# Attention scores as two products over 128 partitions, with the high and low parts stacked inside SBUF

## The chip, the cores and the metric

The kernel runs on one core of one Trainium2 chip. The metric is the device time of one execution in microseconds (us). Before the change the median of three runs is 1916.58 us, the lowest 1916.14 and the highest 1916.92. One execution was also taken by the hardware profiler; its own time is 1916.25 us, and the profile's span, from its first to its last instruction, is 1914.5 us.

## The reference

The program is a small decoder trunk on 512 tokens of width 1024, all in 32-bit floats. Its first layer is a SwiGLU half step, a short gated convolution and a second SwiGLU half step. Keys and values are then projected once from the residual stream. Its second layer is a SwiGLU half step, a causal differential attention over those keys and values, and a last SwiGLU half step. Each sub-layer stands between two RMS norms. The change lies wholly in the attention:

```
k, v = split(rms_norm(x, g_kv) @ w_kv, 2)       # k: 8 heads x 2 x 64,  v: 8 heads x 128
q = (h @ w_q).reshape(b, s, 8, 2, 64) * 64**-0.5
scores = einsum("bqhcd,bkhcd->bhcqk", q, k)     # c = 0, 1: two score matrices in each head
p = softmax(where(causal, scores, -inf))
a = p[:, :, 0] - lam * p[:, :, 1]
o = rms_norm(einsum("bhqk,bkhe->bqhe", a, v), g_subln) * (1 - lambda_init)
m = o.reshape(b, s, 1024) @ w_o
```

So each of the 8 heads has two score matrices of 512 x 512, each a contraction over 64 features; they are masked, normalised row by row, mixed into one matrix, and applied to the head's values.

## The kernel before, in words

**Products in parts.** TensorE multiplies operands of the type fp32r. To keep 32-bit accuracy every operand is held as two tiles: `hi`, the value cast to fp32r by ScalarE (ACT), and `lo`, the remainder, subtracted by VectorE (DVE). The helper `split` (L136) makes both. A product is three matmuls into one PSUM bank: hi by hi, hi by lo, lo by hi (`products`, L143). Weights come in units of 128 x 1024 (512 KB): `unit` (L119) loads a raw tile from the queue of SyncE (SP), ACT casts it to `whi` (L128), DVE subtracts `wlo` (L129). There are two raw tiles, so the load after next waits until DVE has read the raw tile. The pairs `whi`/`wlo` lie in a pool of seven pairs (`wsp`, WUNITS = 7); `pair_of_units` (L112) takes one pair.

**The attention stage.** The queries of all heads are projected first, into the tiles `q`. Then, in `body` (L711 to L750):

- `values(0)` and `values(1)` project the values, four weight units each, 96 matmuls of 512 columns each (L618 to L620).
- `queries(n)` splits one head's queries. It takes a pair from the weight pool: the left halves of the two tiles hold query hi and lo, the right halves will hold key hi and lo.
- `keys(n, k0, k1)` multiplies one weight unit, 24 matmuls of 512 columns for a whole head, and at the end splits the result into the right halves of that pair. In those tiles partitions 0 to 63 belong to the score matrix c = 0 and partitions 64 to 127 to c = 1.
- `scores(n, qt)` makes both score matrices of a block of 128 queries against the keys up to the diagonal, w = (qt + 1) x 128 columns. For each of the three pairs of parts there are two matmuls, one over partitions 0 to 63 and one over 64 to 127 (L653); then one bf16 matmul per matrix adds the causal mask (L655). DVE takes the row maximum (L656), ACT the exponential with the row sum (L661), DVE the reciprocal (L662), ACT scales the second matrix (L665), and DVE mixes the two (L666).
- `turn(n, qt)` transposes the mixed block on TensorE (L678) and splits it; `attend(n)` multiplies it with the values; `sub_norm(n)` normalises the result; `normed` splits it for the output projection.
- `wo.begin(m, ks)` starts column block m of the output projection with the input blocks ks: three matmuls of 512 columns for each.

Before the loop stand values(0), queries(0), keys(0), values(1) and scores(0, 3). Iteration n of the loop makes the keys of head n + 1 in two halves, between them and after them the scores of head n, the transposes, and the attention of head n - 1. The matmuls of the keys, and in the last iteration those of `wo.begin`, are what TensorE has to do while the softmax of a block runs on DVE and ACT. After the loop come the last head, the rest of the output projection and its norm (`closing`, L256).

**What sets the order.** The code names the order in which work is recorded; a scheduler in the tile framework then interleaves the instructions of each engine. What runs on an engine is a fixed list, and each engine works through its list strictly in turn. A tile that is asked for from a pool takes a slot in the order of the code.

## Time and profile before

| what | value |
|---|---|
| median of three runs | 1916.58 us (1916.14 to 1916.92) |
| the profiled execution, its own time | 1916.25 us |
| the profile's span | 1914.5 us |
| TensorE busy over the span | 1895.8 us (99%) |
| DVE, ACT busy over the span | 993.3 us (52%), 739.5 us (39%) |
| granted TensorE clock | 0.999 |

In the views below PE is TensorE's matmuls, PEld its weight loads, SP the queue of SyncE. A row of the timeline gives the start in us, the duration in us, the engine, the line, the operation, output and inputs, the shape and the number of merged instructions, and in brackets how long the engine had been idle and what ended that. A matmul's duration holds the time until its result has left the array; matmuls that follow one another overlap, so the rate is read from the distance between two starts. A row of the table by stretches has the stretch, its length, and for PE, PEld, DVE, ACT and POOL the busy time with the number of instructions, then the granted clock, the DMA share and GB/s.

The stages that the text speaks of, by the trace's own clock: values(0) from 1333.66, keys(0) from 1355.42, values(1) from 1360.86, the first scores at 1382.71, the first transposes at 1390.91, the four transposes of the last head's first block at 1490.65, and the second half of the output projection from 1516.24.

### The profile page before, as it was taken

To read this page: it belongs to the slowest core of one execution; us is meant where nothing else is said; L and a number is where in the kernel's file an instruction comes from. 1 tells how busy PE (TensorE), PEld (TensorE's weight loads), DVE (VectorE), ACT (ScalarE), POOL (GpSimd) and SP (SyncE) were. 2 spreads that over 40 slices of the span, in tenths; PEclk is the share of its full clock that TensorE was granted. 3 is DMA by queue.
4 is the path that set the end of the run, shared out by engine and by line. 5 is a ranking of instruction groups with operands and counts; after the bars stand their busy time and mean duration, and the time that the engine had idled before them with its cause. 6 is when DMAs were issued, how large, how long until landed. Compare 5 with 4: busy or idle time off the path is not lost.

```text
span 1914.5 us, 24288 instructions
## 1 busy us (share of the span) xinstructions
PE 1895.8 (99%) x9780; PEld 1602.9 (84%) x9780; DVE 993.3 (52%) x1673; ACT 739.5 (39%) x1250; POOL 1.1 (0%) x8
## 2 busy tenths in 40 slices
PE   9999999999999999999999999999999999999998
PEld 8888888988898888888988888899866898888886
DVE  7423434574566334344862443457389594234345
ACT  7322222453354322222633222335289673332132
POOL 0000000000000000000000000000000000000000
PEclk9999999999999999999999999999999999999999
DMA  5432323233323323232133332322211224233331
GB/s 167 121 102 90 106 88 103 74 95 94 112 75 104 106 87 101 90 109 89 66 114 100 103 99 95 89 87 92 74 34 61 73 67 132 78 98 100 98 90 65
DMA packets 53664, 178.45 MB, mean 93 GB/s; under 512 B 6320, under 2 KB 9520, under 8 KB 53552
## 3 DMA queue, kind: packets, MB, share of 16 engines
q1 hardware_dynamic: 51632, 174.89, 29.5%
q10 hardware_dynamic: 1920, 2.02, 0.3%
q8 instruction: 77, 1.26, 0.3%
q14 instruction: 35, 0.29, 0.1%
HBM read 174.79 MB, written 2.10 MB: 92 GB/s over the span
## 4 chain that ended last, share of the span: by engine, by line
PE 89%; DVE 7%; ACT 3%; DMA 1%; issue 1%; SPq 0%; DVEq 0%; ACTq 0%
PE acc L147 26%; PE acc L148 26%; PE acc L149 26%; PE d_acc L359 2%; PE d_acc L358 2%; PE d_acc L360 2%; DVE h_lo L221 1%; DVE d L242 1%; DVE x L243 1%; PE v_acc L618 1%; PE v_acc L620 1%; PE v_acc L619 1%; DMA raw<-in_wg 1%; ACT e L661 1%; DVE top L656 1%
## 5 line engine op out<-in xcount | busy, mean ns | idle before, releaser
L147 PE MATMUL acc<-h_hi,whi 128*128 128x512 f32 (+1 forms) x1952 | 697.6, 358 | 4.4 <-ACT whi L128 2.6
L148 PE MATMUL acc<-h_lo,whi 128*128 128x512 f32 (+1 forms) x1952 | 697.6, 358 | 0.1
L149 PE MATMUL acc<-h_hi,wlo 128*128 128x512 f32 (+1 forms) x1952 | 696.3, 357 | 0.0
L128 ACT CAST whi<-raw 128x1024 fp32r<-128x1024 f32 (+2 forms) x336 | 334.4, 1019 | 867.5 <-PE acc L148 718.7
L129 DVE TENSOR_TENSOR wlo<-raw,whi 128x1024 fp32r<-128x1024 f32 (+2 forms) x336 | 396.2, 1182 | 238.8 <-ACT whi L128 237.6
L147 PEld LDWEIGHTS acc<-h_hi,whi 128*128 128x128 f32 x1952 | 367.1, 188 | 59.4 <-ACT whi L128 2.8
L148 PEld LDWEIGHTS acc<-h_lo,whi 128*128 128x128 f32 x1952 | 367.6, 188 | 54.1 <-DVE h_lo L221 0.3
L149 PEld LDWEIGHTS acc<-h_hi,wlo 128*128 128x128 f32 x1952 | 367.3, 188 | 53.7
L410 DVE TENSOR_TENSOR gs<-acc,r 128x512 f32<-128x512 f32 (+1 forms) x100 | 62.5, 625 | 443.8 <-PE acc L149 443.7
L148 PE MATMUL acc<-act_lo,whi 128*128 128x512 f32 (+1 forms) x624 | 223.7, 359 | 0.0
L149 PE MATMUL acc<-act_hi,wlo 128*128 128x512 f32 (+1 forms) x624 | 223.2, 358 | 0.0
L147 PE MATMUL acc<-act_hi,whi 128*128 128x512 f32 (+1 forms) x624 | 223.1, 358 | 0.0
L148 PEld LDWEIGHTS acc<-act_lo,whi 128*128 128x128 f32 x624 | 117.8, 189 | 18.4
L147 PEld LDWEIGHTS acc<-act_hi,whi 128*128 128x128 f32 x624 | 117.4, 188 | 18.0
L149 PEld LDWEIGHTS acc<-act_hi,wlo 128*128 128x128 f32 x624 | 117.3, 188 | 17.7
L138 ACT CAST act_hi<-us 128x512 fp32r<-128x512 f32 (+1 forms) x100 | 56.5, 568 | 64.3 <-DVE us L414 64.3
L358 PE MATMUL d_acc<-whi,act_hi 128*128 128x512 f32 x176 | 68.4, 390 | 0.0
L359 PE MATMUL d_acc<-whi,act_lo 128*128 128x512 f32 x176 | 68.4, 389 | 0.0
L360 PE MATMUL d_acc<-wlo,act_hi 128*128 128x512 f32 x176 | 68.4, 389 | 0.0
L412 DVE TENSOR_TENSOR us<-acc,r 128x512 f32<-128x512 f32 (+1 forms) x100 | 62.5, 625 | 0.0
L141 DVE TENSOR_TENSOR act_lo<-us,act_hi 128x512 fp32r<-128x512 f32 (+1 forms) x100 | 61.7, 620 | 0.7 <-ACT act_hi L138 0.7
L414 DVE TENSOR_TENSOR us<-us,gs 128x512 f32<-128x512 f32 (+1 forms) x100 | 61.5, 620 | 0.4
(156 smaller groups left out, 1646.8 us busy)
## 6 DMA issues: line engine op xcount, KB each, us to landing
raw<-in_wg SPq DMA_DIRECT2D x85, 512.0 KB, 3.8
raw<-in_wu SPq DMA_DIRECT2D x85, 512.0 KB, 3.4
raw<-in_wd SPq DMA_DIRECT2D x48, 448.0 KB, 3.4
raw<-in_wd SPq DMA_DIRECT2D x24, 512.0 KB, 3.8
raw<-in_wci SPq DMA_DIRECT2D x24, 512.0 KB, 3.5
raw<-in_wdt SPq DMA_DIRECT2D x22, 512.0 KB, 3.7
raw<-in_wco SPq DMA_DIRECT2D x8, 512.0 KB, 3.5
raw<-in_wq SPq DMA_DIRECT2D x8, 512.0 KB, 3.4
```

Of the source, the lines that this page charges most:

```text
L128: casts.append(nc.scalar.copy(hi[:, z], raw[:, z]).ins)
L129: nc.vector.tensor_tensor(lo[:, z], raw[:, z], hi.bitcast(F32)[:, z], op=ALU.subtract)
L141: nc.vector.tensor_tensor(dst_lo, src, dst_hi.bitcast(F32), op=ALU.subtract)
L147: nc.tensor.matmul(acc, wh, ah, start=first and j == 0, stop=False)
L148: nc.tensor.matmul(acc, wh, al, start=False, stop=False)
L149: nc.tensor.matmul(acc, wl, ah, start=False, stop=last and j == n - 1)
L358: nc.tensor.matmul(acc, ah, wh, start=k == 0, stop=False)
L359: nc.tensor.matmul(acc, al, wh, start=False, stop=False)
L360: nc.tensor.matmul(acc, ah, wl, start=False, stop=k == m1 - m0 - 1)
L410: nc.vector.tensor_tensor(gs, g, r2[:, p:q], op=ALU.mult)
L412: nc.vector.tensor_tensor(us, up, r2[:, p:q], op=ALU.mult)
L414: nc.vector.tensor_tensor(us, us, gs, op=ALU.mult)
```

## The change

The changed kernel alters four things in the attention and nothing elsewhere.

1. **Scores.** For each score matrix c there is one stacked query tile: query hi in 64 partitions and query lo in the other 64. For the keys there is one tile `kk[n][c]` whose left half is (hi above lo) and whose right half is (lo above hi). A score matrix is then two matmuls over 128 partitions: the first gives hi by hi plus lo by lo, the second hi by lo plus lo by hi. The product lo by lo is thus added, which the kernel before leaves out. The mask matmul now follows each matrix, rather than both.
2. **Stacking.** DMAs from SBUF to SBUF on SP's queue build the stacked tiles: for each head five for the keys (one of 64 x 1024, four of 64 x 512) and three for the queries (64 x 512 each), 64 DMAs in all. Keys are now split into a pair taken from the weight pool at the end of `keys`, queries into tiles of the pool `a`, which grows from 40 to 48 tiles. The room comes from the area reserved for descriptors of software DMAs, which is cut to 512 bytes per partition.
3. **Order of keys and queries.** Keys are made two heads ahead: keys(0) and keys(1) before the loop, keys(n + 2) in iteration n. Queries of heads 0 to 2 are split after keys(0), of heads 3 to 5 after keys(1), of 6 and 7 in iterations 2 and 3.
4. **Output projection.** The parts that are begun early lie in iterations 6 and 7 (4 + 4 and 2 + 2 + 6 input blocks) rather than all in iteration 7 (4 + 2 + 6 + 4).

```
-    apool = ctx.enter_context(tc.tile_pool(name="apool", bufs=5 * NK))
+    apool = ctx.enter_context(tc.tile_pool(name="apool", bufs=SLOTS))      # SLOTS = 48, AHEAD = 6
...
+            up, low = slice(0, HD), slice(HD, P)
+            move = lambda dst, src: nc.sync.dma_start(dst.bitcast(F32), src.bitcast(F32))
             def keys(n, k0, k1):
...
                 if k1 == NK:
-                    split(kq[n][2], kq[n][3], kacc[n])
+                    a, b = kk[n] = pair_of_units("kk")
+                    split(a[:, :S], a[:, S:], kacc[n])
+                    move(b[up], a[low])
+                    for dst, src in ((b[low], a[low]), (a[low], a[up])):
+                        move(dst[:, :S], src[:, S:])
+                        move(dst[:, S:], src[:, :S])
             def queries(n):
-                hi, lo = pair_of_units("kq")
-                kq[n] = [hi[:, :S], lo[:, :S], hi[:, S:], lo[:, S:]]
-                split(kq[n][0], kq[n][1], qs[n])
+                hi, lo = slot(F32R, "qhi"), qs[n].bitcast(F32R)
+                split(hi, lo, qs[n])
+                both = slot(F32R, "qboth")
+                move(both[up], hi[low])
+                move(both[low], lo[low])
+                move(hi[low], lo[up])
+                xs[n] = hi, both
             def scores(n, qt):
...
-                for j, (q, k) in enumerate(((qh, kh), (qh, kl), (ql, kh))):
-                    for cc, s in enumerate(sc):
-                        r = slice(cc * HD, (cc + 1) * HD)
-                        nc.tensor.matmul(s, q[r, qq], k[r, :w], start=j == 0, stop=False)
                 for cc, s in enumerate(sc):
+                    for j in range(2):
+                        nc.tensor.matmul(s, xs[n][cc][:, qq], kk[n][cc][:, j * S : j * S + w], start=j == 0, stop=False)
                     nc.tensor.matmul(s[:, qt * P :], ident16, mask, start=False, stop=True)
...
             values(0, range(NB))
-            queries(0)
             keys(0, 0, NK)
+            for n in range(AHEAD // 2):
+                queries(n)
             values(1, range(NB))
+            keys(1, 0, NK)
+            for n in range(AHEAD // 2, AHEAD):
+                queries(n)
             scores(0, 3)
             for n in range(NH):
-                more = n < NH - 1
-                if more:
-                    queries(n + 1)
-                    keys(n + 1, 0, 4)
+                if n + 2 < NH:
+                    keys(n + 2, 0, 4)
+                if AHEAD <= n + 4 < NH:
+                    queries(n + 4)
                 scores(n, 2)
...
-    nc = bacc.Bacc("TRN2", target_bir_lowering=False, num_devices=1)
+    nc = bacc.Bacc("TRN2", target_bir_lowering=False, num_devices=1, dynamic_dma_scratch_size=SCRATCH)
```

**The order on ACT around the end of keys(0).** `whi` are casts of weight units, numbered by their buffers; `h_hi` splits the normalised input of the keys and values, `v_hi` the values of values(0), `kqhi` or `kkhi` from `k_acc` the keys of head 0. Before the change, where `whi_10970`, `whi_11000`, `whi_11030` and `whi_11060` are the four units of values(1):

```order
L128 CAST whi_10970<-raw_10969 128x1024
L138 CAST h_hi_10700<-xkv_8198 128x512
...
L128 CAST whi_11000<-raw_10999 128x1024
L128 CAST whi_11030<-raw_11029 128x1024
L128 CAST whi_11060<-raw_11059 128x1024
L138 CAST v_hi_10912<-v_acc_10788 128x512
L138 CAST v_hi_10916<-v_acc_10789 128x512
L138 CAST v_hi_10920<-v_acc_10790 128x512
L138 CAST kqhi_11131<-q_10250 128x512
L138 CAST v_hi_10924<-v_acc_10791 128x512
L128 CAST whi_11137<-raw_11136 128x1024
L138 CAST kqhi_10928<-k_acc_10932 128x512
```

With the change, where `whi_10994`, `whi_11024`, `whi_11054` and `whi_11084` are the four units of values(1):

```order
L141 CAST v_hi_10920<-v_acc_10790 128x512
L141 CAST v_hi_10924<-v_acc_10791 128x512
L141 CAST qhi_10968<-q_10249 128x512
L141 CAST qhi_10975<-q_10250 128x512
L141 CAST qhi_10982<-q_10251 128x512
L141 CAST kkhi_10959<-k_acc_10928 128x512
L131 CAST whi_10994<-raw_10993 128x1024
L131 CAST whi_11024<-raw_11023 128x1024
L131 CAST whi_11054<-raw_11053 128x1024
L131 CAST whi_11084<-raw_11083 128x1024
L131 CAST whi_11131<-raw_11130 128x1024
```

All four casts for values(1) stood ahead of the split of head 0's keys; now all four stand behind it.

**The order on PE at the first scores.** `sc` are score matrices, `mask` the mask, `ident` the identity that the mask is multiplied with. Before the change, the block of 512 columns of head 0:

```order
L653 MATMUL sc<-kqhi 128x512 x2
L653 MATMUL sc<-kqlo,kqhi 128x512 x2
L653 MATMUL sc<-kqhi,kqlo 128x512 x2
L655 LDWEIGHTS ident_7892
L655 MATMUL sc<-mask,ident_7892 128x128
L655 LDWEIGHTS ident_7892
L655 MATMUL sc<-mask,ident_7892 128x128
L147 MATMUL k_acc<-h_hi,whi 128x512
```

With the change:

```order
L667 MATMUL sc<-kkhi,qhi 128x512 x2
L668 LDWEIGHTS ident_7892
L668 MATMUL sc<-mask,ident_7892 128x128
L667 MATMUL sc<-kklo,qboth 128x512 x2
L668 LDWEIGHTS ident_7892
L668 MATMUL sc<-mask,ident_7892 128x128
L150 MATMUL k_acc<-h_hi,whi 128x512
L151 MATMUL k_acc<-h_lo,whi 128x512
L667 MATMUL sc<-kkhi,qhi 128x384 x2
```

Six matmuls became four, the mask's two no longer stand side by side, and the next keys are broken off after two matmuls for the next block of scores.

**The order on SP's queue** from the last units of values(1) on, with the change; before it there stood only the rows of weight loads (`raw`), in the same order:

```order
L130 DMA raw<-in_wv 128x1024 x2
L630 DMA qboth<-qhi 64x512
...
L630 DMA kklo<-kkhi 64x512
L630 DMA kklo<-kkhi 64x1024
L630 DMA kklo<-kkhi 64x512
L630 DMA qboth<-q 64x512
L630 DMA qhi<-q 64x512
L630 DMA kkhi<-kkhi 64x512 x2
L130 DMA raw<-in_wv 128x1024 x2
L130 DMA raw<-in_wk 128x1024 x3
```

The loads of the last two units of values(1) and of the keys of heads 1 to 3 moved behind the moves for heads 0 to 2, and the moves wait in the queue for the splits that they copy.

## The prediction

> **What bounds the kernel now.** I read first the busy time of the engines by stretches, cut at the stages of the attention: values(1); from the first transposes to those of the last head's first block (below "the heads"); and from there to the second half of the output projection (below "the tail").

> ```profile
> core 0: us, PE busy (x) PEld busy (x) DVE busy (x) ACT busy (x) POOL busy (x), PEclk, DMA share, GB/s
> 1360.90:1382.70 21.80, 21.80 (x97) 17.80 (x95) 5.74 (x7) 5.51 (x9) 0.00 (x0) 1.00 0.16 49
> 1390.90:1490.70 99.80, 96.42 (x556) 67.78 (x557) 90.40 (x242) 86.95 (x224) 0.00 (x0) 1.00 0.17 54
> 1490.70:1516.20 25.50, 25.17 (x118) 19.05 (x117) 12.60 (x29) 14.68 (x34) 0.00 (x0) 1.00 0.07 22
> ```

> In values(1) and in the tail PE never rests while DVE and ACT have half their time free or more: PE is the bound. In the heads PE shows 97%, but DVE is at 91% and ACT at 87%, each waiting for the other. So I read next what DVE does there, and what its idle time waits for.

> ```profile
> L656 DVE TENSOR_REDUCE top<-sc 128x1 f32<-128x256 f32 (+3 forms) x57 | 26.0, 479 | 1.6 <-PE sc L655 1.6
> L666 DVE SCALAR_TENSOR_TENSOR e<-e,inv 128x384 f32<-128x384 f32 (+3 forms) x28 | 15.1, 548 | 2.4 <-ACT e L665 2.3
> L141 DVE TENSOR_TENSOR aT_lo<-tr,aT_hi 128x512 fp32r<-128x512 f32 (+3 forms) x28 | 13.4, 483 | 1.1 <-ACT aT_hi L138 1.0
> L129 DVE TENSOR_TENSOR wlo<-raw,whi 128x1024 fp32r<-128x1024 f32 x10 | 12.2, 1217 | 0.0
> L662 DVE RECIPROCAL inv<-sums 128x2 f32<-128x2 f32 x28 | 4.2, 158 | 3.7 <-ACT e L661 3.5
> L141 DVE TENSOR_TENSOR kqlo<-q,kqhi 128x512 fp32r<-128x512 f32 x4 | 2.7, 680 | 0.0
> ```

> Of DVE's 99.8 - 90.4 = 9.4 us of idle time, 3.7 + 2.4 + 1.1 = 7.2 wait for ACT inside a softmax, and only 1.6 for PE. In the heads DVE, with its handing to and fro with ACT, is thus nearly as tight as PE, and PE's own gain can't all come through there.

> Third, how PE spends a block of scores: first an undisturbed one, then one into which two transposes were put.

> ```profile
> 1382.39 0.39 PE L620 MATMUL v_acc<-wlo,h_hi 128*128 128x512 f32 x1
> 1382.71 0.50 PE L653 MATMUL sc<-kqhi 64*128 64x512 f32 x2
> 1383.04 0.40 PE L653 MATMUL sc<-kqlo,kqhi 64*128 64x512 f32 x2
> 1383.28 0.40 PE L653 MATMUL sc<-kqhi,kqlo 64*128 64x512 f32 x2
> 1383.61 0.29 PE L655 MATMUL sc<-mask,ident 128*128 128x128 bf16 x2
> 1383.70 0.48 PE L147 MATMUL k_acc<-h_hi,whi 128*128 128x512 f32 x1
> 1384.02 0.40 PE L148 MATMUL k_acc<-h_lo,whi 128*128 128x512 f32 x1
> 1384.25 0.40 PE L149 MATMUL k_acc<-h_hi,wlo 128*128 128x512 f32 x1
> ...
> 1397.76 0.39 PE L149 MATMUL k_acc<-h_hi,wlo 128*128 128x512 f32 x1
> 1398.08 0.44 PE L653 MATMUL sc<-kqhi 64*128 64x384 f32 x1
> 1398.45 0.44 PE L678 MATMUL tr<-ident,e 128*128 128x128 f32 x2
> 1398.82 0.44 PE L653 MATMUL sc<-kqhi 64*128 64x384 f32 x1
> 1398.82 0.61 PE L653 MATMUL sc<-kqlo,kqhi 64*128 64x384 f32 x2
> 1399.11 0.50 PE L653 MATMUL sc<-kqhi,kqlo 64*128 64x384 f32 x2
> 1399.54 0.29 PE L655 MATMUL sc<-mask,ident 128*128 128x128 bf16 x2
> 1399.63 0.48 PE L147 MATMUL k_acc<-h_hi,whi 128*128 128x512 f32 x1
> 1399.95 0.40 PE L148 MATMUL k_acc<-h_lo,whi 128*128 128x512 f32 x1
> ```

> Full products of 512 columns start 0.23 us apart (1384.02, 1384.25). The matmuls over 64 partitions run in pairs, side by side: two start together, the next two 0.24 us on. So the six cost three, not six. But each change between 64 and 128 partitions costs about 0.09 us: 0.32 between 1382.39 and 1382.71 rather than 0.23, the same again before the mask. The queue of weight loads shows why: the load can't run ahead.

> ```profile
> 1382.71 0.19 PEld L653 LDWEIGHTS sc<-kqhi 64*128 64x128 f32 x2 [0.35 <-issue]
> ```

> **The change, part by part.** The sum is made against the profiled execution, 1916.25 us (span 1914.5 and 1.75 around it); it lies 0.33 below the median of 1916.58, less than the runs differ.

> *Scores on PE.* An undisturbed block of 512 columns took, from the end of the stream before (1382.39 + 0.23) to the start of the next (1384.02 - 0.23), 1383.79 - 1382.62 = 1.17 us. The new one has four streams of 0.23, 0.91 us, and two masks, each followed by a full product. The rows show one mask's stream (about 0.06) and the product behind it late by 0.09 (0.32 rather than 0.23), since its weights can't load behind so short a matmul; the two overlap in part, and I take 0.12 for a mask: 0.91 + 0.24 = 1.15. So nearly nothing is won. In a block that transposes break into, the pair falls apart and the modes change twice more: 1399.72 - 1397.99 = 1.73 us. The new one is 4 x 0.175 (three quarters of 0.23) + 0.24 + two transposes of some 0.11 = 1.16: it wins 0.57. Of the 8 blocks of 384 columns the order breaks 6 or 7; for the blocks of 256 and 128 columns, which change mode twice each, I estimate 0.2 per head. PE's own work falls by 6 x 0.57 + 8 x 0.2 + 0.6 = 5.6, say 6 us. Bounds: a loss of 1.7, if a mask between full products costs 0.09 on either side, as a change of rows does, beside its stream of 0.06 (0.24 rather than 0.12, 64 x 0.12 = 7.7 more), and a gain of 10, if the weights on either side of it load unseen (0.06 each). I keep 0.12, the value of the row nearest to it, the mask ahead of `k_acc`.

> [...]

> *The start of values(1): a new wait.* The pair for the keys of head 0 is now taken ahead of the weight pairs of values(1), and the order on ACT puts all four casts behind the split of those keys. That split waits for keys(0), and values(1) waits for the first cast. PE has nothing else in its list.

> ```profile
> 1360.63 0.39 PE L149 MATMUL k_acc<-h_hi,wlo 128*128 128x512 f32 x1
> 1360.86 0.39 PE L618 MATMUL v_acc<-whi,h_hi 128*128 128x512 f32 x1
> ...
> 1349.95 1.05 ACT L128 CAST whi<-raw 128x1024 fp32r<-128x1024 f32 x1 [4.38 <-PE v_acc L619]
> ...
> L138 ACT CAST kqhi<-k_acc x8: 564/586/607, 1361.8 to 1478.4; 128x512 fp32r<-128x512 f32 x8
> L141 DVE TENSOR_TENSOR kqlo<-k_acc,kqhi x8: 679/682/692, 1363.1 to 1479.3; 128x512 fp32r<-128x512 f32 x8
> ```

> Before, the last of these casts began at 1349.95, 11 us ahead, and values(1) followed keys(0) without a gap. Now: keys(0) leave the array at 1361.02, cast 0.59, weight cast 1.05, so PE goes on at 1362.7 rather than 1360.86: 1.8. Two products later (1363.1) it needs `wlo`, 1.22 after the cast, at 1363.9: 0.8. With two handings over, 2.7 us. I see no cover. Bounds 1.8 (if `wlo` comes in time) and 3.5 (if ACT is late at its queue).

> *Keys moved.* keys(1) now stand before the loop: 24 products, 1360.86 - 1355.42 = 5.44 for keys(0), so 5.4 us more ahead of the scores. From there to the first transposes it took 1390.91 - 1382.71 = 8.2 us; now 6 products fewer lie in it (-1.4), but the weights of head 2 are held up behind head 1's split as above, partly covered by scores (0.8 for the cast and 0.5 for `wlo`): 8.1, so -0.1 (between -1.4 and +1.5). In the heads stand 162 products of keys and output projection for 159. The tail has 60 products of the output projection rather than 81, 21 x 0.23 = 4.8 less; it is bound by PE now, but the last head's chain from scores to the projection comes into view there, so I take -4.3 (between -3 and -5.3).

> *The heads.* Counted in the order between the same transposes, DVE has one weight unit more (+1.22), one key split and two query splits less (-0.68 each): 90.4 - 0.8 = 89.6 us. The early query splits help little, since the scheduler had put those of heads 1 to 3 ahead of the scores already. With its 7.2 us of waits for ACT kept and those for PE gone, 96.8; with all its idle time kept, 99.0. PE alone would need less (99.8 - 5). I take 97.3, so -2.5: nearer to the first, as PE comes sooner. Bounds -6.5 (DVE's waits halve as well) and +1.

> *The moves.* 64 DMAs, and SP's loads behind them.

> ```profile
> out_x<-fg SPq DMA_DIRECT2D x8, 256.0 KB, 2.0
> raw<-in_wk SPq DMA_DIRECT2D x8, 512.0 KB, 3.5
> ```

> No row shows a copy inside SBUF. The nearest are a store of 256 KB, 2.0 us, and a load of 512 KB, 3.5. A head's key moves are two rounds, the second waiting for the first: 4 to 7 us. Head 1's stacked keys, the tightest, are wanted some 10 us after their split, the others 14 or more: hidden, 0. If a round takes 3.5, head 1 is late by 0 to 1. The third unit of values(1) is now loaded behind head 0's moves, at about 1366.5, and split by 1372.3 (3.5 + 1.05 + 1.22); PE wants it two units after the late start, at 1374.3. Cover 2 us; if the moves take longer than that, PE waits for the rest. What is late next is the weight unit of the next keys, cast only after a head's keys are split: some 4 us of scores, norm and transposes cover 0.59 + 1.05 + 1.22 = 2.9 us of work, with a third of a microsecond to spare where other work stands between. [...]

> The sum: +2.7 + 5.4 - 0.1 - 2.5 - 4.3 = +1.2, so 1917.45 us, in round numbers 1917.4: no change that can be told. About 0.2%, 3.8 us, is what a measurement of this kernel can tell from none; the chances below go by it.

> **The rivals.** *Faster, 1911.9 us.* The heads run at PE's pace after all: DVE's waits for ACT overlap once scores come early. Then the heads shrink by PE's 6 us and by the 1.6 that DVE waits for PE, to -8 instead of -2.5, and the sum is -4.3. For it: PE's 97% there stands above DVE's 91%. Against it: only 1.6 us of DVE's idle time wait for PE, and the uneven load, since two of the seven stretches between heads now hold six of eleven weight units.

> *Slower, 1923 us: the masks.* A bf16 matmul between fp32r products costs 0.09 on either side, as a change of rows does now. PE then loses 1.7, the heads go from -2.5 to +1.8, start and tail lose 1.3: 1.2 + 4.3 + 1.3 = +6.8. It decides from 0.18 us per mask on. Against it: transposes and products, which differ in type too, follow each other at 0.11.

> *Slower, 1921 us: weights late.* A wait of 0.7 us at each of the five key units of the heads, since their cast is tied to the split before them or their load to the moves: +3.5 on the sum, 1920.9. For it: the spare third of a microsecond. Against it: loads are issued some 10 us before.

> *It does not do what it says.* If stacked tiles came later than 10 us, scores(1, 3) would hold up PE: a round of 5 us each way would cost 2 to 4 us once. The order shows the two products themselves.

> **How the numbers follow.** Forecast 0.48, faster 0.30, masks 0.08, late weights 0.11, late stacks 0.03. The forecast's own range is 1914 to 1920.5. Of its 0.48, 0.40 lie within 0.2%, 0.04 on either side; of the faster rival 0.27 are faster and 0.03 not, of the others 0.18 slower and 0.04 not. Faster 0.31, same 0.47, slower 0.22. For 8 in 10 the range goes to 1910 and to 1922.

> **What would show it.** The scores' rows with 128*128 and 0.23 us apart, masks with 0.12 behind them; a wait of 2 to 3 us of PE for the cast at the start of values(1); the heads at 96 to 99 us with DVE above 91%; the tail near 21 us. Wrong it would be with the heads under 94 us (DVE was not the bound), with waits of PE for stacked tiles or for `whi` in each iteration, or without the wait at values(1).

## The result, and the profile after

The changed kernel takes 1927.32 us (median of four runs, 1926.82 to 1927.74), the kernel before, on the same chip, 1916.46 us (four runs, 1916.14 to 1916.92): a ratio of 1.0056, 95% interval 1.0039 to 1.0074. The change makes the kernel slower by about 11 us; the forecast was 1917.4, and its range ended at 1922. The profile's span grew from 1914.5 to 1925.0 us.

The same stages first, as busy time by stretches of the changed kernel: from values(0) to the first scores, to the first transposes, from there to head 5's, to head 7's, and to the second half of the output projection. The columns are start and end, length, busy time of PE, PEld, DVE, ACT and POOL with the number of instructions, the granted clock, the DMA share and GB/s.

```profile
1332.78:1389.09 56.31, 54.69 (x241) 44.97 (x240) 20.85 (x28) 15.67 (x25) 0.00 (x0) 1.00 0.38 108
1389.09:1396.67 7.58, 7.02 (x34) 5.04 (x33) 5.69 (x14) 4.80 (x11) 0.00 (x0) 1.00 0.78 184
1396.67:1464.94 68.27, 66.27 (x356) 50.26 (x356) 58.84 (x162) 56.19 (x149) 0.00 (x0) 1.00 0.46 116
1464.94:1504.14 39.20, 30.79 (x147) 23.17 (x147) 32.31 (x79) 32.46 (x78) 0.00 (x0) 0.83 0.31 90
1504.14:1523.64 19.50, 16.87 (x81) 12.82 (x80) 10.44 (x25) 10.48 (x24) 0.00 (x0) 1.00 0.15 50
```

The same five of the kernel before:

```profile
1333.66:1382.71 49.05, 49.05 (x218) 40.37 (x216) 19.72 (x25) 15.37 (x24) 0.00 (x0) 1.00 0.27 84
1382.71:1390.91 8.20, 8.09 (x44) 5.65 (x43) 6.06 (x13) 4.46 (x11) 0.00 (x0) 1.00 0.21 65
1390.91:1461.64 70.73, 68.59 (x395) 48.65 (x396) 63.03 (x171) 61.34 (x159) 0.00 (x0) 1.00 0.14 46
1461.64:1490.65 29.01, 27.77 (x162) 19.07 (x162) 27.31 (x72) 25.55 (x66) 0.00 (x0) 1.00 0.23 74
1490.65:1513.01 22.36, 22.11 (x106) 16.74 (x105) 11.67 (x27) 13.05 (x32) 0.00 (x0) 1.00 0.07 24
```

| stage | before | after | difference | predicted |
|---|---|---|---|---|
| start, values(0) to first scores | 49.05 | 56.31 | +7.26 | +8.1 (2.7 + 5.4) |
| to the first transposes | 8.20 | 7.58 | -0.62 | -0.1 |
| heads, first five stretches | 70.73 | 68.27 | -2.46 | |
| heads, last two stretches | 29.01 | 39.20 | +10.19 | heads in all -2.5 |
| tail | 22.36 | 19.50 | -2.86 | -4.3 |

Less the 0.9 us by which the stage starts earlier in this execution, that is, to within 0.2, the 10.5 us of the span. (The tail is cut here at the first product of 256 columns; by the prediction's cut, 3 to 4 us later, it goes from 25.6 to 23.2, -2.4.) Start, transposes and tail each lie within 2 us of the forecast. The first five stretches alone won what was forecast for all seven; that is chance, since the forecast wasn't split by stretches. The fourth row, the stretches of the last two heads, holds the miss. PE is busy there for 30.79 of 39.20 us, and the granted clock is 0.83, where it is 1.00 before. Its idle time has grown from 1.2 to 8.4 us, its busy time by 3.0.

What PE did in the middle of it, by the timeline of the changed kernel (start, duration, instruction, and in brackets the idle time before it and what ended that):

```profile
1472.05 0.40 PE L151 MATMUL acc<-on_lo,whi 128*128 128x512 f32 x1
1475.50 0.69 PE L691 MATMUL tr<-ident,e 128*128 128x128 f32 x2 [3.06 <-DVE n_q L184]
1478.53 0.45 PE L691 MATMUL tr<-ident,e 128*128 128x128 f32 x1 [2.34 <-DVE inv L675]
1479.33 0.79 PE L702 MATMUL oacc<-aT_hi,v_hi 128*128 128x512 f32 x1 [0.35 <-ACT aT_hi L141]
1479.92 0.63 PE L150 MATMUL acc<-on_hi,whi 128*128 128x512 f32 x1
1480.35 0.63 PE L703 MATMUL oacc<-aT_lo,v_hi 128*128 128x512 f32 x1
```

PE's list has two products of the output projection there and then transposes, which stand still for 3.06 and 2.34 us until DVE is done. And behind the two waits products of 512 columns start 0.43 us apart (1479.92, 1480.35), not 0.23 as at the full clock (1388.64, 1388.87): the clock has halved. The granted clock of two stretches in which PE doesn't rest, the first behind these waits and the second behind two shorter ones (1.23 and 1.03 us, with one transpose between them), shows it:

```profile
1479.33:1484.29 4.96, 4.96 (x13) 4.19 (x14) 4.07 (x8) 2.30 (x6) 0.00 (x0) 0.50 0.41 122
1498.35:1501.18 2.83, 2.83 (x8) 2.54 (x9) 2.64 (x8) 2.83 (x8) 0.00 (x0) 0.50 0.00 0
```

At the full clock these 7.8 us of products would have taken half as long: an estimate of 3.9 us for what the clock costs PE directly. DVE in the same moment:

```profile
1473.89 0.69 DVE L144 TENSOR_TENSOR on_lo<-o,on_hi 128x512 fp32r<-128x512 f32 x1
...
1474.76 0.68 DVE L184 SCALAR_TENSOR_TENSOR n_q<-otot,n_q 128x512 f32<-128x512 f32 x1
1475.36 0.68 DVE L144 TENSOR_TENSOR on_lo<-o,on_hi 128x512 fp32r<-128x512 f32 x1
1475.96 0.69 DVE L185 SCALAR_TENSOR_TENSOR ro<-n_q,n_y 128x512 f32<-128x512 f32 x1
1476.56 0.69 DVE L144 TENSOR_TENSOR on_lo<-o,on_hi 128x512 fp32r<-128x512 f32 x1
...
1477.82 0.56 DVE L144 TENSOR_TENSOR aT_lo<-tr,aT_hi 128x384 fp32r<-128x384 f32 x1
```

DVE works without a gap, and `n_q`, which frees the PSUM buffer that the transposes wait for, stands among the splits of the output projection's inputs (`on_lo`): `normed(0, 1, 2, 3)` is recorded in one piece. The groups of DVE in these two stretches, after, with count, busy time and mean ns:

```profile
L132 DVE TENSOR_TENSOR wlo<-raw,whi 128x1024 fp32r<-128x1024 f32 x6 | 7.3, 1217 | 1.2 <-ACT whi L131 1.2
L144 DVE TENSOR_TENSOR on_lo<-o,on_hi 128x512 fp32r<-128x512 f32 x6 | 4.1, 687 | 0.3 <-ACT on_hi L141 0.3
```

and before:

```profile
L129 DVE TENSOR_TENSOR wlo<-raw,whi 128x1024 fp32r<-128x1024 f32 x4 | 4.9, 1220 | 0.0
L141 DVE TENSOR_TENSOR on_lo<-q,on_hi 128x512 fp32r<-128x512 f32 x3 | 2.0, 681 | 0.0
```

Two weight units and three of these splits more, 4.5 us, now lie in these two stretches (and one split of keys fewer), and less work in the five ahead of them. ACT's work in these two has grown as well, by 6.9 us (32.46 against 25.55).

The other steps, in rows of the changed kernel. The new wait at the start of values(1), by the timeline:

```profile
1359.75 0.39 PE L152 MATMUL k_acc<-h_hi,wlo 128*128 128x512 f32 x1
1361.76 0.50 PE L621 MATMUL v_acc<-whi,h_hi 128*128 128x512 f32 x1 [1.62 <-ACT whi L131]
...
1363.48 0.39 PE L622 MATMUL v_acc<-whi,h_lo 128*128 128x512 f32 x1
1363.71 0.62 PE L623 MATMUL v_acc<-wlo,h_hi 128*128 128x512 f32 x2
```

and the scores:

```profile
1389.09 0.61 PE L667 MATMUL sc<-kkhi,qhi 128*128 128x512 f32 x2
1389.55 0.23 PE L668 MATMUL sc<-mask,ident 128*128 128x128 bf16 x1
1389.59 0.71 PE L667 MATMUL sc<-kklo,qboth 128*128 128x512 f32 x2
```

Two products take 1389.55 - 1389.09 = 0.46 us, as forecast; the mask follows at once, and the first of the two products behind it takes some 0.09 more (the next mask starts at 1390.14, 0.55 behind 1389.59).

### The profile page after: what moved, and what is told of

The parts are those of the page before. It is cut to its first block, busy times and chain, and to the rows that moved or that the text cites. A ratio compares the mean times of both kernels' runs of the same rounds, so it can differ in the third digit from the quotient of the medians.

```text
span 1925.0 us, 24264 instructions
## 1 busy us (share of the span) xinstructions
PE 1896.1 (98%) x9716; PEld 1608.2 (84%) x9716; DVE 994.0 (52%) x1673; ACT 739.0 (38%) x1250; POOL 1.1 (0%) x8
## 3 DMA queue, kind: packets, MB, share of 16 engines
q10 hardware_dynamic: 1920, 2.02, 0.3%
## 4 chain that ended last, share of the span: by engine, by line
PE 90%; DVE 5%; ACT 3%; issue 1%; DMA 1%; SPq 0%; DVEq 0%; ACTq 0%
PE acc L150 26%; PE acc L151 26%; PE acc L152 26%; PE d_acc L361 2%; PE d_acc L362 2%; PE d_acc L363 2%; DVE h_lo L224 1%; ACT e L674 1%; DVE x L246 1%; PE v_acc L621 1%; PE v_acc L623 1%; PE v_acc L622 1%; DVE d L245 1%; PE tot L204 1%; PE k_acc L150 1%
## 5 line engine op out<-in xcount | busy, mean ns | idle before, releaser
L141 ACT CAST act_hi<-us 128x512 fp32r<-128x512 f32 (+1 forms) x100 | 56.5, 568 | 64.4 <-DVE us L417 64.4
## 6 DMA issues: line engine op xcount, KB each, us to landing
raw<-in_wg SPq DMA_DIRECT2D x85, 512.0 KB, 3.9
raw<-in_wu SPq DMA_DIRECT2D x85, 512.0 KB, 3.4
raw<-in_wd SPq DMA_DIRECT2D x24, 512.0 KB, 3.8
raw<-in_wci SPq DMA_DIRECT2D x24, 512.0 KB, 3.5
raw<-in_wdt SPq DMA_DIRECT2D x22, 512.0 KB, 3.7
raw<-in_wco SPq DMA_DIRECT2D x8, 512.0 KB, 3.5
raw<-in_wq SPq DMA_DIRECT2D x8, 512.0 KB, 3.4
```

## The experiments

The theory after the result, **A**: the new order piles DVE's and ACT's work up in the stretches of the last heads; transposes wait there, and the halved clock behind the waits adds to it. The rival, **B**: the stacked scores themselves (masks between full products, moves that land late) cost the time.

**One part each.** `order_only` keeps the changed order, but makes the scores as before:

```diff
-                    a, b = kk[n] ... split(a[:, :S], a[:, S:], kacc[n]); move(...) x 5
+                    split(a[:, :S], b[:, :S], kacc[n])
-                    for j in range(2): matmul(s, xs[n][cc][:, qq], kk[n][cc][:, j * S : j * S + w], ...)
+                    for j, (q, k) in enumerate(((qh, kh), (qh, kl), (ql, kh))):   # 64 partitions each
```

> The changed kernel's order alone: keys two heads ahead, queries with the values, the output projection begun in iterations 6 and 7, but scores as six matmuls over 64 partitions and no moves. Theory A: the pile-up is still there, the stretches from head 5 to head 7 take 35 us or more (29.0 before, 39.2 with the change), and the time is 1924 to 1931. Theory B: 1915 to 1919, as the stacked scores are gone.

Measured: 1926.74 us, ratio 1.0057 (1.0042 to 1.0072), where the changed kernel has 1927.32. Stretches of its heads:

```profile
1396.38:1468.11 71.73, 68.55 (x397) 48.07 (x396) 58.75 (x162) 57.42 (x152) 0.00 (x0) 1.00 0.11 38
1468.11:1504.56 36.45, 31.77 (x151) 21.39 (x151) 31.64 (x77) 30.04 (x74) 0.00 (x0) 0.86 0.28 87
```

Without stacks and without moves the loss is there in full (10.9 us against the kernel before on the same chip, as with the whole change): the order alone makes it. The stacked scores gain 3.5 us in the first five stretches (71.73 against 68.27) and lose 2.8 in the last two (36.45 against 39.20); why they lose them there was not tried. B falls as the cause.

`scores_only` is the opposite: stacks and moves, but the loop of before, with keys one head ahead.

```diff
-            keys(1, 0, NK)            # ahead of the loop, keys(n + 2, ...) in it
+            # keys(n + 1, ...) in the loop, as in the kernel before
```

> The changed kernel's stacked scores and their moves, with the order of the kernel before: keys one head ahead, each head's queries split one head ahead, the output projection begun in the last iteration alone. Theory A (the loss is a pile-up of DVE and ACT work in the stretches from head 5 to head 7, made by the new order): the seven stretches between heads come to 96 to 101 us, as before the change (99.7), and the time to 1914 to 1920. Theory B (the loss comes from the stacked scores themselves, by masks or by moves that land late): the loss stays, 1924 or more, and PE waits for stacked keys in every iteration.

Measured: 1967.67 us, ratio 1.0268 (1.0253 to 1.0284). Theory A's number for it was wrong by some 50 us, and by the words of the expectation the run came out as B. Its heads, by stretches (first five, last two):

```profile
1392.33:1497.36 105.03, 74.82 (x340) 55.33 (x340) 64.43 (x165) 57.85 (x151) 0.00 (x0) 0.81 0.29 78
1497.36:1542.67 45.31, 33.55 (x154) 25.32 (x153) 33.84 (x79) 33.17 (x79) 0.00 (x0) 0.81 0.37 103
```

and one iteration of it, by the timeline of PE:

```profile
1416.97 0.49 PE L691 MATMUL tr<-ident,e 128*128 128x128 f32 x3
1420.43 0.41 PE L691 MATMUL tr<-ident,e 128*128 128x128 f32 x2 [2.97 <-DVE e L679]
1422.65 0.47 PE L691 MATMUL tr<-ident,e 128*128 128x128 f32 x1 [1.81 <-DVE n_q L184]
1423.72 0.77 PE L667 MATMUL sc<-kkhi,qhi 128*128 128x512 f32 x1 [0.59 <-DMA kkhi<-kkhi]
```

The last moves of the keys are issued at 1419.96 (SP's queue) and PE's scores wait for them until 1423.72. Everything that used to cover the softmax now stands behind these scores: six transposes stand in a row ahead of them, and PE has 6.7 us in which it does nothing else. In six places PE waits 0.6 to 2.4 us right ahead of stacked scores, 9 us in all, and for 33 us DVE is what its transposes wait for; the granted clock is 0.81. That is B's mechanism, but not the changed kernel's, where no wait of PE for a move stands in the heads. So keys two heads ahead are no ornament of the change, they are the price of the stacks.

**The small mendings.** `units_first` takes the units of values(1) from the pool ahead of keys(0):

```diff
+            for kk4 in range(NK // 2):
+                vu[1, kk4] = unit(i["wv"][1][:, kk4 * 1024 : (kk4 + 1) * 1024], 1024)
             keys(0, 0, NK)
```

> The changed kernel with the four weight units of values(1) taken from their pool ahead of keys(0), so that their casts can stand ahead of the split of head 0's keys. If the place in the pool makes the wait at the start of values(1): the wait of 1.9 us goes and nothing else moves, 1925.0 to 1926.0. If the wait only moves to another place: 1927 to 1928.

Measured: 1925.62 us (1.0051, 1.0036 to 1.0066). The wait is gone, and the start falls from 56.31 to 54.40 us: 1.9 us, about the size of the wait (the forecast had 2.7).

`norm_spread` splits one head's normed output in each of iterations 2 to 5, not four in iteration 5:

```diff
-                if n == 5:
-                    normed(0, 1, 2, 3)
+                if 2 <= n <= 5:
+                    normed(n - 2)
```

> The changed kernel with the splits of the first four normalised heads spread over iterations 2 to 5, one each, rather than four in iteration 5. Theory A: the two stretches from head 5 to head 7 shrink from 39.2 to 30 to 34 us, TensorE's clock stays full there, and the time is 1917 to 1922. Theory B, or if the weight units rather than the splits make the pile: 1925 to 1928, the stretches still 37 or more.

Measured: 1923.37 us (1.0037, 1.0025 to 1.0050). Its heads, first five stretches and last two:

```profile
1397.50:1467.65 70.15, 66.03 (x356) 49.84 (x356) 60.34 (x165) 58.74 (x155) 0.00 (x0) 1.00 0.42 113
1467.65:1501.48 33.83, 27.88 (x136) 21.02 (x136) 29.66 (x73) 28.53 (x70) 0.00 (x0) 0.91 0.35 101
```

5.4 us less in the last two, 1.9 more in the five ahead of them, which have no room for the work. The stretches are as theory A had them, but not the clock (0.91), and the time lies between the two expectations.

**The clock.** `warm` gives PE something to do where it waits: products whose result nobody uses, in a PSUM bank of their own, in iterations 5 and 6.

```diff
+                if n in (5, 6):
+                    busy = ps.tile([P, S], F32, tag="ps", name="busy")
+                    for z in range(4):
+                        nc.tensor.matmul(busy, halves[D], x[:, z, :], start=z == 0, stop=z == 3)
                 turn(n, 1)
                 turn(n, 0)
```

> The changed kernel and, besides, in iterations 5 and 6 ahead of the second turn of transposes, four products of 512 columns whose result nobody uses, in a PSUM bank of its own: work for PE in the place where it waits for VectorE. If the granted clock of 0.6 to 0.7 there, which comes after PE's waits, adds to the loss (products 0.43 to 0.59 us apart rather than 0.23), the clock stays nearer to 1.0 and the last two stretches fall from 39.2 us by 2 to 5, to a time of 1922 to 1925. If the clock only follows the waits and costs nothing of its own, the two stretches stay at 39 or grow by the added products, up to 2 x 4 x 0.9 us at the rate of plain fp32, and the time is 1927 to 1934.

Measured: 1921.85 us (1.0032, 1.0019 to 1.0045), 5.5 us below the changed kernel, although it does more; each against the kernel before on its own chip, the loss falls from 10.9 to 6.3 us. The last two stretches:

```profile
1466.16:1499.77 33.61, 31.29 (x153) 21.19 (x152) 30.93 (x75) 29.70 (x72) 0.00 (x0) 1.00 0.39 118
```

The clock is back at 1.00 and the stretches fall from 39.20 to 33.61. So the clock behind the waits costs time of its own. That all of the 5.6 us are the clock isn't shown: by the rows above it costs 3.9 directly, and the added products changed PE's list too (twelve products of the output projection now run from 1476.40 to 1479.77, ahead of a transpose behind which they stood before). DVE is now busy for 30.93 of 33.61 us, 92%, nearly as before (27.31 of 29.01, 94%), with 3.6 us more to do than before; but PE is busy for 31.29, 7.4 of them with the added products, so which of the two holds the remaining 4.6 us the run can't say.

**The pile.** `nolo` leaves out the low part of the output projection's weights:

```diff
+            if rest:                       # rest=False for the units of wo; hi stands in for lo
                 nc.vector.tensor_tensor(lo[:, z], raw[:, z], hi.bitcast(F32)[:, z], op=ALU.subtract)
```

> The changed kernel without the low part of the output projection's weights: their subtraction on VectorE is left out, and the high part stands in its place in the products, so PE, ACT and the loads have the same work. It takes 1.2 us of VectorE for each weight unit of the output projection, six of which (7.3 us) lie in the last two stretches. Theory A (pile of VectorE's work): the two stretches fall from 39.2 to 31 to 34 us and the time to 1919 to 1922. If the wait comes from somewhere else (stacked keys, loads, ACT): the two stretches stay above 37 and the time is 1925 to 1927.

Measured: 1922.45 us (1.0033, 1.0020 to 1.0045); the last two stretches fall to

```profile
1466.30:1501.87 35.57, 30.40 (x140) 21.90 (x140) 25.53 (x71) 31.32 (x76) 0.00 (x0) 0.86 0.37 111
```

which is between the two expectations: 6.8 us less of DVE buy 3.6 us. The splits of the norm and ACT's casts are still there, PE still waits, and the clock is still low. What it waits for has changed, though: in the changed kernel DVE ended 6.6 us of PE's waits in these stretches and ACT 1.8, here DVE 0.9 and ACT 4.0. `nolo_warm` makes both edits.

> The edits of the runs nolo and warm together: the low part of the output projection's weights left out (its products take the high part in its place), and the unused products of 512 columns in iterations 5 and 6. The last two stretches took 39.2 us in the changed kernel, 33.6 in warm at a granted clock of 1.0 and 35.6 in nolo at 0.86. Theory A with the clock (a pile of VectorE's work makes PE wait, and the clock that falls behind it makes the rest): with both taken away the two stretches come to PE's own work with the added products, 29 to 31.5 us, the clock stays at 1.0, and the time is 1918 to 1920.5. If something else holds them up (ScalarE, which is busy for 31 us of nolo's two stretches): they stay at 32.5 to 34 us and the time at 1921 to 1923.

Measured: 1923.67 us (1.0037, 1.0023 to 1.0051), no better than either; the stretches and the time are above both expectations, nearer to the one that names ScalarE. The last two stretches:

```profile
1466.22:1500.69 34.47, 32.36 (x148) 22.39 (x148) 25.60 (x69) 30.03 (x72) 0.00 (x0) 0.95 0.37 115
```

PE is busy for 32.36 of 34.47 us, and without the added products it would have about 7 us less to do: they are now a bound themselves. The run doesn't tell the theories apart, and `nolo_spread` was made for that: `nolo`, `norm_spread` and `units_first` together, nothing added.

> The changed kernel without the low part of the output projection's weights (the high part stands in its place in the products), with the norm of heads 0 to 3 one head at a time in iterations 2 to 5, and with the units of values(1) ahead of keys(0); no added products. If the pile is the weight units' low parts and the norm's splits together (both queued ahead of the transposes' splits): the waits of 2 to 4 us and the clock below 1.0 are gone without any filling, the last two stretches take 28 to 31 us, the five ahead of them 70, and the time is 1916 to 1919. If the pile is something else (the exponentials' chain itself, with less of PE's work beside it): the last two stretches stay above 33 us with waits and a clock near 0.9, and the time is 1920 to 1923.

Measured: 1920.71 us (1.0024, 1.0015 to 1.0033).

```profile
1395.68:1465.80 70.12, 66.03 (x356) 49.87 (x356) 60.28 (x165) 58.70 (x155) 0.00 (x0) 1.00 0.42 113
1465.80:1496.09 30.29, 26.46 (x135) 19.77 (x135) 23.70 (x68) 28.20 (x70) 0.00 (x0) 0.94 0.42 131
```

The stretches are as expected, 30.3 and 70.1: with the weights' low parts and the norm's splits out of the way, all but 1.3 of the 10.2 us is gone from the last two, with no filling (1.9 us went to the five ahead of them). The clock is 0.94 and not 1.00, and PE still waits for 2.9 us on ACT and 0.7 on DVE. The time isn't as expected, since the expectation forgot what stands outside: the heads are 100.4 us in all, those of before 99.7 (with the low parts made), and the start is still 5.4 us longer while the tail gives back 2.0.

**Spreading it, and fewer keys ahead.** `spread` distributes the keys evenly over iterations 0 to 5, the norm over 2 to 5, and begins the output projection later; `half` makes keys only one and a half heads ahead:

```diff
+            first_half, second_half = (4, 4, 4, 4, 4, 3, 4, 0), (4, 4, 4, 3, 3, 3, 0, 0)   # spread: key blocks
-            keys(1, 0, NK)
+            keys(1, 0, 4)              # half; keys(n + 1, 4, NK) and keys(n + 2, 0, 4) in the loop
```

> Edits to the changed kernel: the norm of heads 0 to 3 in iterations 2 to 5, one head each, instead of all four in iteration 5; the four units of values(1) taken ahead of keys(0); the keys of heads 2 to 7 spread evenly over iterations 0 to 5; the output projection begun later, its first group in iteration 6, the second and third in iteration 7. The scores, the moves and keys(1) ahead of the loop stay. Theory A (the loss is a pile of work for VectorE in the stretches of the last three heads, made by the order): those two stretches fall from 39.2 to 30 to 32 us, the start of values(1) gives back its 1.9, the five stretches ahead of them stay at 68 to 70, and the time is 1917 to 1920. Theory B (a pile isn't the cause; whatever comes later than those places in the new order waits all the same): the two stretches stay above 36 us and the time is above 1922.

> As the run spread in its norm, the units of values(1) and the late output projection, but keys one and a half heads ahead rather than two: only the first half of keys(1) stands before the loop, and iteration n makes the second half of keys(n+1) and the first half of keys(n+2). 12 products of 0.23 us, 2.7 us, go from ahead of the loop into the loop, where PE has time to spare if VectorE is its bound. If the stacked keys still land in time: 2 to 3 us less from values(0) to the first scores than in spread, and a time 0 to 3 us below it, 1915 to 1919. If they land late, as with keys one head ahead (some 6.7 us of waits a head there): waits of PE at the first scores of each head, 2 to 4 us a head, and a time of 1930 to 1945.

Measured: 1925.94 us for `spread` (1.0054, 1.0039 to 1.0069) and 1924.24 for `half` (1.0046, 1.0031 to 1.0061). In `spread` the last two stretches took 31.1 us, as A said, but the five ahead of them 75.0, not 68 to 70. Two of these:

```profile
1436.20:1452.88 16.68, 12.61 (x55) 8.78 (x56) 13.30 (x38) 13.20 (x36) 0.00 (x0) 0.80 0.32 85
1452.88:1470.65 17.77, 15.94 (x84) 12.16 (x82) 13.81 (x36) 12.27 (x32) 0.00 (x0) 0.90 0.28 73
```

The waits went elsewhere and took the low clock with them (0.80 and 0.90): in these two stretches PE now waits 4.0 us for DVE and 1.9 for casts of weight units. `half` starts 2.7 us earlier than `spread`, as expected (51.68 us to the first scores), and its stacks land nearly in time (1.2 us of waits for them in all). Its heads take 105.8 us, as those of `spread` do (106.1), so that 1.7 us of the gain stay; the range of 1915 to 1919 was too low because it started from the time that was expected of `spread`.

**The best of it.** `combo` is `units_first`, `norm_spread` and `warm` together, `combo_two` the same with two added products each time instead of four.

> The changed kernel with the three small mendings together: the units of values(1) ahead of keys(0), the norm of heads 0 to 3 one head at a time in iterations 2 to 5, the unused products of iterations 5 and 6. If they add up (1.9 from the first, and warm's two stretches with a part of the norm's 0.7 us a head moved ahead of them): 1918 to 1920.5. It stays above the kernel before, 1916, in either case, since 5.4 us of keys(1) stand ahead of the loop and the tail gives back 2.5 of them and the first stretches 0.6 to 2.5.

> The run combo with two added products instead of four in each of iterations 5 and 6 (1.8 us of PE each time rather than 3.5). If the added products in combo were longer than the waits that they cover: the last two stretches fall from 33.1 to 30 to 32 us and the time from 1920.2 to 1918 to 1919.5. If two are too few to hold the clock: the clock falls to 0.9 there and the time is 1920 to 1923.

Measured: 1920.16 us (1.0023, 1.0014 to 1.0032) and 1921.37 us (1.0024, 1.0015 to 1.0033). In `combo_two` the last two stretches are no shorter than in `combo` (33.12 and 33.14 us), at a clock of 0.95 instead of 1.00: two are too few to hold the clock, and four cost what they save beyond that. `combo` is the best version of the changed kernel that was found, 7 us below it and still 0.23% above the kernel before.

**Work for GpSimd.** `before_pool` and `pool` make the low parts of the output projection's weights on GpSimd, which is idle (POOL 0.00 us in every stretch above), in the kernel before and in the changed one (with `units_first` and `warm`).

```diff
-            nc.vector.tensor_tensor(lo[:, z], raw[:, z], hi.bitcast(F32)[:, z], op=ALU.subtract)
+            engine.tensor_tensor(...)      # engine = nc.gpsimd for the units of wo
```

> The kernel before with the low part of the output projection's weights made on GpSimd, and nothing else changed. Three to four of them lie in its heads, 1.2 us of VectorE each. If VectorE is the bound of the heads there, as the prediction had it, they fall from 99.7 by 1 to 3 us and the time is 1913 to 1915. If PE is the bound: no change, 1915.5 to 1917. If GpSimd is too slow: PE waits for low parts in the tail, 1917 to 1925.

> The changed kernel with the units of values(1) ahead of keys(0), the unused products of iterations 5 and 6, and the low part of the output projection's weights made on GpSimd instead of VectorE, nothing left out. If VectorE's work is the bound of the last two stretches and GpSimd makes a low part in less than 4 us without holding up the others: the two stretches come to 29 to 31.5 us, and the time to 1916 to 1918.5. If GpSimd is slower than that, or VectorE gets slower beside it: PE waits for low parts, and the time is 1920 to 1930.

Measured: 1931.89 us for `before_pool` (1.0081, 1.0067 to 1.0094) and 1928.01 for `pool` (1.0059, 1.0046 to 1.0071): slower, both. GpSimd needs 2.40 us for a unit where DVE needs 1.22, which alone would be covered. But by the timeline of `before_pool`, GpSimd's first

```profile
1451.57 2.40 POOL L130 TENSOR_TENSOR wlo<-raw,whi 128x1024 fp32r<-128x1024 f32 x1 [1449.93 <-DVE top L657]
```

and DVE beside it and beside a later pair of them (1469.30 to 1474.00)

```profile
1451.67 2.85 DVE L142 TENSOR_TENSOR on_lo<-q,on_hi 128x512 fp32r<-128x512 f32 x1
...
1469.44 2.24 DVE L658 TENSOR_SCALAR neg<-top 128x2 f32<-128x2 f32 x1
1471.60 0.28 DVE L657 TENSOR_REDUCE top<-sc 128x1 f32<-128x128 f32 x1
1471.91 2.12 DVE L658 TENSOR_SCALAR neg<-top 128x2 f32<-128x2 f32 x1
```

show a split of 0.68 us that takes 2.85, and a scaling of two columns, 0.16 us elsewhere, that takes 2.24 and 2.12, until GpSimd's instruction is over. The row maximum out of PSUM between them takes its usual 0.28. Over the last three stretches (1446 to 1502), thirteen such scalings took 0.94 us each, 0.16 before: 10.1 us lost, for 7.3 spared by six subtractions. That DVE's work is the bound in these stretches could not be tried in this way.

## Why the prediction was wrong

**The heads: the step that failed.** The prediction summed DVE's work over the seven stretches (89.6 us, against 90.4 before), kept its waits, and got 97.3 us, -2.5. (Of the 7.2 us that it put down to ACT, its rows give ACT 6.8.) Measured are 107.5 us, +7.7, outside the bounds (-6.5 to +1). Its count of DVE's work was off by only 1.6: 58.84 + 32.31 = 91.2 us, which is 0.8 more than before, not 0.8 less. And the sign that it named, DVE above 91% in the heads, came out as 85%. What was wrong is the sum over all seven, as if work could be done wherever there is room. In the first five stretches PE is the bound after the change (66.27 of 68.27 us, DVE at 86%), and what DVE has less to do there isn't won. In the last two DVE has 5.0 us more to do than before, and PE no more products of keys and output projection to fill the time with (37 against 39). The text even held the uneven load, "two of the seven stretches between heads now hold six of eleven weight units", but as an argument against the faster rival and without a price. Priced by its own rows, two units of 1.22 and three splits of 0.68 more in two stretches at 94% make 4.5 us there, a little under half of the 10.2.

**The clock: a term that wasn't in the sum.** No term of the prediction, and no rival, let the granted clock change, since all stages showed 1.00. In the changed kernel it falls to 0.83 over the last two stretches, where products at half the clock cost some 3.9 us by their rows; `warm`, which holds it at 1.00, takes 5.6 us off them, in part by another list of PE. If each counts in full, the 4.5 us of work and the 3.9 make 8.4 of the 10.2; how the rest divides is open. In the trace the granted clock is 0.50, and products of 512 columns are 0.43 us apart for 0.23, behind waits of 3.06 and 2.34 us with two transposes between them, and behind waits of 1.23 and 1.03 us with one. How long a wait must be for that no run shows.

**The start: right in kind, mis-sized by 0.8.** keys(1) ahead of the loop cost 5.4, as said. The wait at values(1) was there, for the cast named, with 1.8 us of the 1.8 forecast for it (the products would have gone on at 1359.98 and did at 1361.76). What wasn't there are the 0.8 us for `wlo`: the sum let PE ask for it after two products, but the order puts eight with `whi` first (1361.76 to 1363.71), and it comes in time. `units_first` removes just the 1.9. From there to the first transposes -0.6 for -0.1, within its bounds.

**Scores and moves: right.** 0.46 us for two products, and about 0.12 for a mask with the product behind it. As far as it can be seen, PE gained what was said; `order_only` shows 3.5 us of the 6 in the first five stretches and that it changes nothing in the time (1926.74 against 1927.32). The moves are hidden in the changed kernel: no wait of PE for them stands in its heads. The cover named, 10 us and more between a head's split and its scores, comes with the distance of two heads; with one head, in `scores_only`, PE waits for the stacks.

**The tail: right in sign, -2.9 for -4.3.** 21 products fewer were to give 4.8, less 0.5 for the last head's chain. That chain comes into view more than that: a transpose waits 2.6 us for a split of DVE's.

```profile
PE tr L691 <- DVE aT_lo L144: 2.6, 1, 2.6
```

**The rivals.** None of the slower ones was the one that came. Masks cost what the forecast said; no weight unit was late by 0.7 in each iteration; the stacks were in time. The faster one named what happens in the first five stretches (PE's pace), and lost it in the last two. What was missing is a rival of the kind "work is moved from where DVE has room to where it has none".

**What was not settled.** That the order makes the loss is shown by `order_only`, and that less work in the last two stretches takes most of it away by `norm_spread`, `nolo` and `nolo_spread`. How DVE and ACT share it is not settled. `nolo` takes 6.8 us of DVE's work and 1.1 of ACT's from these stretches and wins 3.6 us; `norm_spread` takes only 2.7 of DVE's, but 3.9 of ACT's, and wins 5.4. In both, and in `nolo_spread`, the larger part of PE's remaining waits ends with ACT, which is busy for 28.20 of the 30.29 us in `nolo_spread`, while DVE has 3.6 us less to do there than in the kernel before. So ACT's work is a part of the pile, and no run took work from ACT alone.

## What to carry to other kernels

Sum each engine's work by the stretch in which it must be done, never over a stage: moving work that costs nothing in total moved the bound from one engine to another, stretch by stretch, and won nothing in the one while it lost in the other. Waits of PE of 1 to 3 us in close succession cost more than themselves here, since the granted clock was 0.50 behind them and the products of 512 columns that followed came 0.43 us apart for 0.23; look for such waits in a new order, and price the products behind them too. And a gain on an engine that shares the bound with another (here four matmuls in place of six, forecast at 6 us of PE) must first pay for the order that it needs: keys two heads ahead cost 5.4 us at the start, of which the tail gave back 2.9.

## What the runs showed of the hardware

```profile
kklo<-kkhi SPq DMA_DIRECT2D x16, 128.0 KB, 2.6
kkhi<-kkhi SPq DMA_DIRECT2D x16, 128.0 KB, 3.5
```

  Two rounds, the second behind the first, are thus some 6 us from a split to a stacked tile, within the 4 to 7 that were taken.
- A small instruction of DVE took nearly the whole of a GpSimd instruction beside it (2.24 us for 0.16, beside 2.35, in `before_pool`), and a split 2.85 us for 0.68 beside 2.40. The row maximum from PSUM between two such scalings took its usual 0.28.
